# Attention maps turned by VectorE's 32x32 blocks and a round trip through DRAM, and the matrix engine's order around them written out by hand

## The chip, the cores and the metric

The kernel runs on one core of one Trainium2 chip. Times are device microseconds of the whole program on that core, taken over several executions; the profile shows one execution, instruction by instruction. The engines of the core work side by side, each through its own queue in order: TensorE (PE, with its weight loads as PEld), VectorE (DVE), ScalarE (ACT), GpSimd (POOL) and SyncE (SP), which here only issues transfers. A transfer can be issued from SP's, ACT's or POOL's queue; all of them end on the same 16 DMA engines.

## The reference, cut to what matters

Two layers, 256 tokens, width 1024, all in float32. Each layer normalises x, projects it, runs two token mixers, gates and merges them and projects back:

```python
proj = h @ w_in[l]                       # q_a k_a v_a ab z_a | q_b k_b v_b z_b | gate_a gate_b
y_a = gated_delta_branch(q_a, k_a, v_a, ab_a, z_a, ...)     # 8 heads of 128, both directions
# differential attention, 8 heads, two score maps of 64 channels each:
p = softmax(s); a = p[0] - lam * p[1]    # 256 x 256 for each head
o = einsum('bhqk,bhkd->bhqd', a, v)
y_b = rmsnorm(o) * (1 - lambda_init) * silu(z_b)
merged = sigmoid(gate_a) * (y_a @ w_pa[l]) + sigmoid(gate_b) * (y_b @ w_pb[l])
x = x + merged @ w_out[l]
```

The change concerns the map `a` of each head. It is made with queries on the partitions, but the product `a @ v` contracts over keys, so the map has to be turned before TensorE can use it.

## The kernel before, in words

**Projections.** The 256 tokens are two tiles (`m`) of 128. A projection of 512 columns (`proj_tm`, L315) runs over eight k-tiles of 128; each takes six matmuls of 512 columns: high x high, high x low and low x high part of the operands, for both token tiles. I call these six a **step**. Weights arrive in four loads of 512 KB a projection (`weights`, L273), each for two steps, on SP's queue (L304); ACT writes the rounded high part (L308), DVE the rest (L310). There are three buffers for raw weights and two each for the high and low parts, so each load waits until DVE is done with an older one.

**The stretch that the change is in.** In each layer, after the projections for q, k and v, TensorE works through ten projections of eight steps: zb0, zb1, za0, za1 (steps 0 to 31), gb0, gb1 (32 to 47), ga0, ga1 (48 to 63), pb0, pb1 (64 to 79). `place(at)` (L1158) names the last matmul of step `at`. Other work is put between these steps:

- **Attention.** `scores(h)` (L1053) makes the two score maps of head h at steps 3, 7, 11 ... 31; DVE takes the row maxima (L1069), ACT the exponentials and their sums (L1071), DVE combines the two maps (L1077) into `es[:, 0]`. `turn(h)` (L1081) turns the map: four TensorE transposes of 128x128 (L1088) into one PSUM bank and an ACT copy to `aT` (L1090). `attend(h)` (L1093) multiplies it with v (L1099). Turn and product of head h-1 stand beside the scores of head h, four steps later; head 7's stand at steps 34 and 39.
- **The delta rule's triangular inverse.** `substitute` (L865) solves 32x32 blocks on DVE (L870, L871), spread over the projections. `spread_blocks` (L873) makes a transposed copy (L874) and sends both to DRAM through POOL's queue (L878, `udr`). `merges(g)` (L897) for two groups g of four heads loads them back as `T64` (L905: group 0 through POOL's queue, group 1 through SP's) and into `U_` (L909, POOL's queue), and merges the blocks on TensorE from step 41 on (`y64p`, L923). `chunks(g)` (L976) follows from step 52 to 68.
- **Gating of the attention's output.** `gate_yb(i)` (L1236) scales half i of the heads (L1191), and `send`/`fetch` (L247, L254) turn it by DVE's block transpose (L249) and DRAM; `split_B` (L259) makes high and low parts for `pb`. It stands at the end of gb1 (i = 0) and at the end of ga0 (i = 1).

**What sets the order.** A scheduler orders each engine's instructions by priority in a simulated run. `behind(ins)` (L270) keeps an instruction behind another on its engine; `tc.high_priority` lifts it. TensorE's order between the steps comes from such pins and priorities.

**Buffers that matter.** `es` has two buffers (tag "w4a"), `aT` two (tag "w2a", L1084), score banks from head 2 on are the two of `ps_c`, turned maps and products with v use the two banks of `ps_m`. `ob` and the ga tiles share tag "eo", `vb` and the gb tiles share "ev".

**The turn by DVE and DRAM** already exists for v (`turn_squares` and `bounce`, L133 and L137): DVE transposes the 32x32 blocks in place, one transfer writes 256 KB to DRAM, four transfers of 64 KB read it back with the blocks in their new places, all on POOL's queue.

Of the kernel before, what the change touches and what calls it, by code (L numbers as in the profile page):

```python
# [17 lines left out]
P = 128  # L18
DM = 1024
KT = DM // P  # L20
SEQ = 256
# [28 lines left out]
def hybrid_encoder(  # L50
# [53 lines left out]
    mark = {}  # L104
# [53 lines left out]
    def norm_row(w_row, nm):  # L158
# [14 lines left out]
        for i in range(3):  # L173
            mm = T.matmul(wb[i > 0], one if i else tri[:, 0, :], hl[:, i - 1] if i else row,
                          start=i < 2, stop=i != 1)
            tc.keep_in_program_order(mm)
# [138 lines left out]
    def proj_tm(act, w, c0, n, evac, nm, places=(None,) * 4, spare=(), later=None, turned=(), between=None,  # L315
# [3 lines left out]
        for kt, hi, lo in weights(w, c0, n, nm, places, later=later, spare=spare, turned=turned, held=held,  # L319
                                  first=first, raws=raws):  # L320
            for m in range(NM):
                ts_ = slice(m * P, (m + 1) * P)
                o = accs[m][:, :n]
                T.matmul(o, act[kt // 4][:, 0, kt % 4, ts_], hi, start=kt == 0, stop=False)  # L324
                T.matmul(o, act[kt // 4][:, 0, kt % 4, ts_], lo, start=False, stop=False)  # L325
                mark["proj"] = T.matmul(o, act[kt // 4][:, 1, kt % 4, ts_], hi, start=False,  # L326
                                        stop=kt == KT - 1).ins
                mark["done", nm, kt] = mark["proj"]
        if between:
            between()  # L330
        for m in range(NM):
            evac(m, accs[m][:, :n])
# [76 lines left out]
    for _ in range(5):  # L409
        mm = T.matmul(idle[:, :P], ones, ones, start=True, stop=True)  # L410
        tc.keep_in_program_order(mm)
# [22 lines left out]
    for m in range(NM):  # L434
        mm = T.matmul(pos_p[:, m : m + 1], pos_r[:, m * P : (m + 1) * P], ones[0:1, 0:1], start=True, stop=True)
        mark["pos"] = mm.ins
        tc.keep_in_program_order(mm)
# [69 lines left out]
    for l in range(DEPTH):  # L507
# [86 lines left out]
        def qk_part(s_, i):  # L594
                def evac_qk(m, ps):
# [11 lines left out]
                    for b in range(4):  # L607
# [4 lines left out]
                proj_tm(hT, wl, (C_QB, C_KB)[s_] + 512 * i, 512, evac_qk, f"qk{l}{s_}{i}",  # L612
                        turned=(0, 1) if (s_, i) == (0, 1) else ())
# [170 lines left out]
        def gram(nm, g, c, slot, after=None):  # L784
            gp = (bank if slot else bank_c)(f"{nm}{l}{g}{c}")
            for j4 in range(4):
                kqh = kq[:, 4 * g + j4, c]
                with behind(after):
                    mark[nm, g, c] = T.matmul(gp[:, j4 * P : (j4 + 1) * P], kqh[:, 0, :], kqh[:, slot, :],
                                              start=True, stop=True).ins  # L790
# [35 lines left out]
        def weigh_q(g, c, after):  # L826
            bv = B[:, c, 4 * g : 4 * g + 4]
            with tc.high_priority(offset=HP):
                gp = gram("kq", g, c, 1, after)
# [554 lines left out]
```

## Time and profile before

| | us |
|---|---|
| median of three runs | 750.23 |
| fastest and slowest run | 749.87, 751.79 |
| the profiled execution, first to last instruction (its span) | 748.5 |

The profile gives a span and no time of its own for the execution that it shows; the median stands 1.7 us over that span.

| engine | busy us | share of span | instructions |
|---|---|---|---|
| PE (matmul) | 739.3 | 99% | 5176 |
| DVE | 586.5 | 78% | 1109 |
| ACT | 481.2 | 64% | 1022 |
| POOL | 139.5 | 19% | 221 |

In a view of groups, a row reads: line, engine and operation, result and operands, shape, count, then busy time in us and mean ns of one. A timeline row reads: start, duration, engine, line, operation, count, and in brackets the idle time before it and what ended it. In a table by stretch each engine's busy time is followed by its count, then the granted clock of TensorE, the DMA engines' busy share and GB/s. Matmul records overlap (each is shown with its run through the array), so what one costs in a stream is read from the distance between starts.

### The profile page before, as it was taken

Reading aid. Unit: us, or ns where it says so; the run is one execution under the profiler, and the core shown is the slowest. Engines: PE = TensorE matmul, PEld = TensorE weight load, DVE = VectorE, ACT = ScalarE, POOL = GpSimd, SP = SyncE. Lnnn points to the kernel's source line nnn. Section 1 sums busy time; section 2 is a strip of 40 time slices with the busy share of each in tenths; the row PEclk is TensorE's granted clock in tenths of the full one; section 3 lists DMA queues with packets and bytes.
Section 4 is the critical chain, followed back from the end, with each engine's and each line's share of the span. In section 5 each row is a group of like instructions: output and inputs, shape, how many; then the busy total and the mean of one; then the engine's idle time right before and its main releaser. Section 6 shows DMA issues by size and latency. Waiting matters only on the chain.

```text
span 748.5 us, 13917 instructions
## 1 busy us (share of the span) xinstructions
PE 739.3 (99%) x5176; PEld 641.7 (86%) x5176; DVE 586.5 (78%) x1109; ACT 481.2 (64%) x1022; POOL 139.5 (19%) x221
## 2 busy tenths in 40 slices
PE   8999999999999999999999999999999999999996
PEld 6999889987888889888889899889778888998885
DVE  8696898999985965578668779999999679537782
ACT  6757875667876576645456578555687757566552
POOL 6004110112023440100000150202110425301000
PEclk9999999999999999999999999999999999999999
DMA  8754566776667462567674466767666748335641
GB/s 260 239 170 169 170 179 198 209 211 193 208 177 186 145 184 84 171 200 247 199 232 133 128 192 180 219 176 230 195 171 195 197 133 229 95 114 201 220 141 57
DMA packets 73734, 135.46 MB, mean 181 GB/s; under 512 B 12944, under 2 KB 13921, under 8 KB 73666
## 3 DMA queue, kind: packets, MB, share of 16 engines
q1 hardware_dynamic: 64750, 113.65, 50.6%
q0 software_dynamic: 7936, 19.35, 8.7%
q10 hardware_dynamic: 980, 1.58, 0.6%
q8 instruction: 41, 0.67, 0.4%
q14 instruction: 27, 0.22, 0.1%
HBM read 125.53 MB, written 9.01 MB: 180 GB/s over the span
## 4 chain that ended last, share of the span: by engine, by line
PE 95%; ACT 2%; issue 1%; DVE 1%; DMA 1%; SPq 0%; POOLq 0%; POOL 0%; DVEq 0%; ACTq 0%
PE pp_vb L369 4%; PE pp_qk L325 4%; PE pp_qk L326 3%; PE pp_qk L324 3%; PE sc L1061 2%; PE pp_o L369 2%; PE pf_k L385 2%; PE pp_za L325 2%; PE pf_v L385 2%; PE pf_v L389 2%; PE pp_gb L324 2%; PE pp_gb L325 2%; PE pp_zb L324 2%; PE pf_q L387 2%; PE pf_k L387 2%; PE pf_v L387 2%
## 5 line engine op out<-in xcount | busy, mean ns | idle before, releaser
L325 PE MATMUL pp_qk<-lo_qk,hT 128*128 128x512 f32 x128 | 50.5, 395 | 0.3
L326 PE MATMUL pp_qk<-hi_qk,hT 128*128 128x512 f32 x128 | 50.0, 390 | 0.0
L310 DVE TENSOR_TENSOR lo_qk<-raw_qk,hi_qk 128x1024 fp32r<-128x1024 f32 x32 | 39.1, 1222 | 11.6 <-ACT hi_qk L308 11.4
L324 PE MATMUL pp_qk<-hi_qk,hT 128*128 128x512 f32 x128 | 45.1, 393 | 0.0
L308 ACT CAST hi_qk<-raw_qk 128x1024 fp32r<-128x1024 f32 x28 | 29.4, 1049 | 23.4 <-PE pp_qk L326 12.4
L1071 ACT ACTIVATE es<-sc,mx 128x256 f32<-128x256 f32 x64 | 29.6, 474 | 19.5 <-DVE mx L1069 19.5
L387 PE MATMUL pf_q<-hT,hi_q 128*128 128x256 f32 x128 | 36.1, 286 | 0.0
L385 PE MATMUL pf_k<-hT,hi_k 128*128 128x256 f32 x128 | 36.1, 287 | 0.0
L385 PE MATMUL pf_v<-hT,hi_v 128*128 128x256 f32 x128 | 35.9, 285 | 0.0
L387 PE MATMUL pf_v<-hT,hi_v 128*128 128x256 f32 x128 | 35.8, 284 | 0.0
L385 PE MATMUL pf_q<-hT,hi_q 128*128 128x256 f32 x128 | 35.8, 284 | 0.0
L387 PE MATMUL pf_k<-hT,hi_k 128*128 128x256 f32 x128 | 35.8, 284 | 0.0
L310 DVE TENSOR_TENSOR lo_pb<-raw_pb,hi_pb 128x1024 fp32r<-128x1024 f32 x16 | 19.6, 1225 | 20.5 <-ACT hi_pb L308 20.2
L389 PE MATMUL pf_q<-hT,lo_q 128*128 128x256 f32 x128 | 35.2, 288 | 0.0
L389 PE MATMUL pf_v<-hT,lo_v 128*128 128x256 f32 x128 | 34.6, 288 | 0.0
L389 PE MATMUL pf_k<-hT,lo_k 128*128 128x256 f32 x128 | 34.3, 284 | 0.0
L308 ACT CAST hi_pa<-raw_pa 128x1024 fp32r<-128x1024 f32 x16 | 16.8, 1053 | 22.3 <-PE pp_pa L326 16.1
L679 DVE SCALAR_TENSOR_TENSOR cvq<-pf_q,cw,cvq 128x254 f32<-128x254 f32 (+1 forms) x64 | 30.0, 479 | 0.9 <-ACT cvq L675 0.3
L679 DVE SCALAR_TENSOR_TENSOR cvv<-pf_v,cw,cvv 128x254 f32<-128x254 f32 (+1 forms) x64 | 30.1, 482 | 0.1
L679 DVE SCALAR_TENSOR_TENSOR cvk<-pf_k,cw,cvk 128x254 f32<-128x254 f32 (+1 forms) x64 | 29.0, 478 | 1.3 <-ACT cvk L675 0.6
L325 PEld LDWEIGHTS pp_qk<-lo_qk,hT 128*128 128x128 f32 x128 | 24.0, 188 | 6.6 <-DVE lo_qk L310 1.6
L310 DVE TENSOR_TENSOR lo_pa<-raw_pa,hi_pa 128x1024 fp32r<-128x1024 f32 x16 | 19.6, 1224 | 11.1 <-ACT hi_pa L308 11.1
(414 smaller groups left out, 2542.2 us busy)
## 6 DMA issues: line engine op xcount, KB each, us to landing
raw_qk<-in_w_in_dram SPq DMA_DIRECT2D x32, 512.0 KB, 3.8
raw_k<-in_w_in_dram SPq DMA_DIRECT2D x16, 512.0 KB, 4.7
raw_q<-in_w_in_dram SPq DMA_DIRECT2D x16, 512.0 KB, 3.7
raw_v<-in_w_in_dram SPq DMA_DIRECT2D x16, 512.0 KB, 3.8
raw_zb<-in_w_in_dram SPq DMA_DIRECT2D x16, 512.0 KB, 3.7
raw_za<-in_w_in_dram SPq DMA_DIRECT2D x16, 512.0 KB, 3.7
raw_ga<-in_w_in_dram SPq DMA_DIRECT2D x16, 512.0 KB, 4.4
raw_pb<-in_w_pb_dram SPq DMA_DIRECT2D x16, 512.0 KB, 3.8
```

What stands on the lines that cost most here:

```text
L308: high = (V.tensor_copy if kp in turned else S.copy)(hi[:, :, :n], raw[:, :, :n]).ins
L310: mark[nm, kp] = high, V.tensor_tensor(lo[:, :, :n], raw[:, :, :n], hi[:, :, :n].bitcast(F32), ALU.subtract).ins
L324: T.matmul(o, act[kt // 4][:, 0, kt % 4, ts_], hi, start=kt == 0, stop=False)
L325: T.matmul(o, act[kt // 4][:, 0, kt % 4, ts_], lo, start=False, stop=False)
L326: mark["proj"] = T.matmul(o, act[kt // 4][:, 1, kt % 4, ts_], hi, start=False, stop=kt == KT - 1).ins
L369: mark["proj"] = T.matmul(o, act[kt // 4][:, pa, kt % 4, ts_], ws[kt][1 + pw], start=kt == 0 and n_ == 0, stop=kt == KT - 1 and n_ == 2).ins
L385: T.matmul(o, hi[:, cs], act[kt // 4][:, 0, kt % 4, :], start=first, stop=False, skip_group_check=True)
L387: T.matmul(o, hi[:, cs], act[kt // 4][:, 1, kt % 4, :], start=False, stop=False, skip_group_check=True)
L389: T.matmul(o, lo[:, cs], act[kt // 4][:, 0, kt % 4, :], start=False, stop=done, skip_group_check=True)
L679: V.scalar_tensor_tensor(ca[:, o0:o1], acc[:, b, o0 + sft : o1 + sft], cw[:, j, cb : cb + 1], ca[:, o0:o1], ALU.mult, ALU.add)
L1061: mm = T.matmul(sp[n][:, qt * SEQ : (qt + 1) * SEQ], qkT[h // 4][rows, 0, h % 4, qt * P : (qt + 1) * P], qkT[h // 4][rows, 1, h % 4, :], s ...
L1071: S.activation(es[:, n, qt, :], spv[:, qt, :], AF.Exp, bias=mx[:, n, qt : qt + 1], accum_out=s_all[:, h, n, qt : qt + 1])
```

## The change

It does four things.

1. `turn` no longer uses TensorE. DVE transposes the map's 32x32 blocks into `es[:, 1]`, a transfer writes 256 KB to DRAM (`att`), and four transfers of 64 KB read it back as `aT`, all on POOL's queue, each kept behind the one before (`mark["queued"]`). The two query tiles lie interleaved, so TensorE reads the weights of `a @ v` with a step of two elements.
2. `a @ v` of head h stands at steps 20, 24, 28, 32, 36, 40, 43, 46, the scores at steps 6, 10 ... 34, so fourteen steps lie between them for heads 0 to 5, thirteen and twelve for the last two.
3. From zb0 to the end of pb1 every matmul made through `mm` is put behind the one before it; `drive` runs the projections step by step and runs the jobs that `plan` has put after a step. The steps of the merges, the chunk work and `weigh_q` keep their numbers.
4. `T64` of both groups and `U_` are loaded through SP's queue. `gate_yb(0)` and `gate_yb(1)` are issued at steps 54 and 58.

```diff
+    def mm(*args, **kw):
+        if mark["chain"] is None:
+            return T.matmul(*args, **kw)
+        with behind(mark["chain"]):
+            made = T.matmul(*args, **kw)
+        mark["chain"] = made.ins
+        return made
...
             for b in range(4):
                 co = 32 * (b % 2)
-                (nc.sync if g else G).dma_start(out=T64[blk(b), :, co : co + 32],
-                                                in_=udr[1, b, g].rearrange("t j i -> j t i"))
+                nc.sync.dma_start(out=T64[blk(b), :, co : co + 32],
+                                  in_=udr[1, b, g].rearrange("t j i -> j t i"))
             yield
             for b in range(4 if g == 0 else 0):
-                G.dma_start(out=U_[blk(b), :, :, blk(b)].rearrange("j g t i -> j (g t) i"),
+                nc.sync.dma_start(out=U_[blk(b), :, :, blk(b)].rearrange("j g t i -> j (g t) i"),
                                   in_=udr[0, b].rearrange("g t j i -> j (g t) i"))
...
-        def turn(h, es, at):
-            with tc.high_priority(offset=HP):
-                ap_ = bank(f"at{l}{h}")
-                aT = work.tile([P, NM, SEQ], F32, tag="w2a", name=f"aT{l}{h}", bufs=2)
-                for qt in range(NM):
-                    for kt in range(NM):
-                        with behind(at):
-                            mark["at", h] = T.transpose(ap_[:, kt * SEQ + qt * P : kt * SEQ + (qt + 1) * P],
-                                                        es[:, 0, qt, kt * P : (kt + 1) * P], ident).ins
-                S.copy(aT.rearrange("p k q -> p (k q)"), ap_)
-            return aT
...
+        def turn(h, es):
+            V.transpose(es[:, 1].rearrange("p k (j t q) -> p (k j) q t", j=4, q=2),
+                        es[:, 0].rearrange("p q (x t) -> p x q t", t=32))
+            dd = dram.tile([NM, 4, 32, 4, 64], F32, tag="att", name=f"att{l}{h}", bufs=4)
+            with behind(mark.get("queued")):
+                G.dma_start(out=dd.rearrange("k i t j r -> (i t) k (j r)"), in_=es[:, 1])
+            back = work.tile([P, NM, 4, 64], F32, tag="w2a", name=f"aT{l}{h}", bufs=2)
+            for j in range(4):
+                with behind(mark.get("queued")):
+                    mark["queued"] = G.dma_start(out=back[blk(j)].rearrange("t k i r -> t (k i) r"),
+                                                 in_=dd[:, :, :, j].rearrange("k i t r -> t (k i) r")).ins
+            aT[h] = back
+
+        def attend(h):
+            op_ = bank(f"av{l}{h}")
+            av = aT[h].rearrange("p k i (t q) -> p q k (i t)", q=2)
+            for qt in range(NM):
+                for kt in range(NM):
+                    mm(op_[:, qt * P : (qt + 1) * P], av[:, qt, kt],
+                       vb[h // 4][:, kt, h % 4 * P : h % 4 * P + P],
+                       start=kt == 0, stop=kt == NM - 1)
...
+        def attention(h):
+            turn(h, scores(h))
+
+        def drive(gens, first):
+            for n, gen in enumerate(gens):
+                for kt in range(KT):
+                    next(gen)
+                    for job in jobs.get(KT * (first + n) + kt, ()):
+                        job()
...
+        for h in range(NH):
+            plan((6, 10, 14, 18, 22, 26, 30, 34)[h], attention, h)
+        for h in range(NH):
+            plan((20, 24, 28, 32, 36, 40, 43, 46)[h], attend, h)
+        mark["chain"] = mark["proj"]
...
+            at = [mark[f"ga{l}1", m][1] if i else mark[f"ga{l}0", 2 + m][1] for m in range(NM)]
...
+        for n, at in enumerate((39, 42, 44, 47)):
+            plan(at, weigh_q, n // 2, n % 2)
         order = [(mg, 41), (mg[:1], 43), (mg[1:], 45), (mg, 48), (mg, 50)]
         order += [(ch[i : i + 1], at + i) for at in (52, 54, 57, 59, 62, 64, 67) for i in range(2)]
...
+        plan(54, gate_yb, 0)
+        plan(58, gate_yb, 1)
```

More of the change, by code (lines that the diff above doesn't have):

```diff
@@ L1093, in attend @@
[L1093 to L1101 removed]
+        aT = {}
@@ L1227, in hybrid_encoder @@
[L1227 to L1235 removed]
+        gtb, gta = [], []
@@ L1279, in hybrid_encoder @@
             gated(osb, za, ro, nw[:, 0:1], yaT, f"ya{l}", (m,))
-        branch(yaT, w_pa[l], gta, f"pa{l}")
+        for i in range(2):
+            full(branch(yaT, w_pa[l], gta, f"pa{l}", i))
         mT = pair(f"mT{l}")
```

225 lines of the change are left out of this document (93 added, 132 removed).

## The prediction, made before the change was run

> **What bounds the kernel now.** I read the page's busy times and chain first, then the table by stretch around the attention of layer 0, then the chain piece by piece there.
>
> ```profile
> span 748.5 us, 13917 instructions
> ...
> PE 739.3 (99%) x5176; PEld 641.7 (86%) x5176; DVE 586.5 (78%) x1109; ACT 481.2 (64%) x1022; POOL 139.5 (19%) x221
> ...
> PE 95%; ACT 2%; issue 1%; DVE 1%; DMA 1%; SPq 0%; POOLq 0%; POOL 0%; DVEq 0%; ACTq 0%
> 160.00:210.00 50.00, 50.00 (x266) 39.52 (x265) 48.28 (x107) 38.88 (x104) 5.46 (x10) 1.00 0.62 184
> 210.00:240.00 30.00, 30.00 (x164) 24.83 (x162) 20.62 (x37) 21.65 (x56) 9.27 (x16) 1.00 0.71 197
> 270.00:310.00 40.00, 40.00 (x284) 37.02 (x282) 17.46 (x34) 25.64 (x59) 7.57 (x11) 1.00 0.39 121
> ```
>
> The chain that ended last is TensorE for 95% of the span. In the three stretches it is busy all the time at the full granted clock (1.00). So a matmul taken out is worth its place in TensorE's stream, as long as nothing else becomes late. What could is also there: from 160 to 210 us DVE is busy 48.28 of 50 us, and the change gives DVE more to do just there. From 210 on DVE has room (20.62 of 30, then 17.46 of 40).
>
> **The transposes that go.** The chain shows what each instruction adds to the stream:
>
> ```profile
> 176.88 0.23 PE pp_zb L324
> 177.11 0.44 PE at L1088 x4
> 177.55 0.24 PE pp_zb L325
> ```
>
> A head's four transposes take 0.44 us between matmuls of 0.23. Eight heads in two layers: 16 x 0.44 = **7.0 us** off TensorE. A step is six matmuls, 6 x 0.23 = 1.4 us. Scores and products with v keep their number, so moving them costs nothing in itself; forcing the order by hand costs nothing where the data is there, and all of a wait where it is not, since TensorE cannot pass over.
>
> **The reads with a step of two elements.** No row shows TensorE reading weights so. The nearest rows are ACT and DVE with a step of four elements (16 bytes):
>
> ```profile
> L263 ACT ACTIVATE ybT<-zb,nw 128x512 fp32r<-128x512 f32 x8 | 9.9, 1241 | 0.0
> ...
> L1090 ACT COPY aT<-at 128x512 f32<-128x512 f32 x16 | 9.4, 585 | 0.0
> ...
> L244 ACT ACTIVATE yaT<-pt_ya,nw 128x512 fp32r<-128x512 f32 x8 | 5.1, 682 | 0.0
> L249 DVE STREAM_TRANSPOSE zb<-ob 128x512 f32<-128x512 f32 x8 | 8.4, 1092 | 0.1
> ...
> L135 DVE STREAM_TRANSPOSE tb_v<-thv 128x512 f32<-128x512 f32 x8 | 5.7, 712 | 0.0
> 204.61 0.89 PE av L1099 x8
> ...
> 212.68 0.89 PE av L1099 x8
> ```
>
> ACT's strided read (L263) takes 1.82 times the dense one from PSUM (L244); DVE's strided write (L249) 1.53 times the dense one (L135). A head's product is eight instructions in 0.89 us, 0.111 each, 128 in both layers. Bounds: 0, or 128 x 0.111 x 0.82 = 11.6 us. I see no reason for a gain. I take 0, because the step here is half of that in the slow rows, and keep 11.6 for the range. [...]
>
> **DVE and ACT.** DVE gains 16 block transposes with a write step of two: between the 0.712 us of L135 and the 1.092 of L249. I take 0.72, nearer to the dense row for the same reason as above; 5.8 us a layer. ACT loses 16 copies (L1090), 9.4 us; it was not full (38.88 of 50), so that is worth nothing. From 160 to 210 some six of the eight maps of a layer fall in: 48.28 + 6 x 0.72 = 52.6 us of work for 50 us, and TensorE wants to be through sooner. Something must slip. It need not be the weights: the block substitution is the work with time in hand, so what it feeds is late next (below). For casts that come late for TensorE the bounds are 0 and the excess of 2.6 us a layer; I take 0.4, 0.8 us in all.
>
> **The round trip.** That for v shows its length:
>
> ```profile
> 166.92 0.56 POOL L140 DMA_DIRECT2D bnc_v<-tb_v  x1 [11.61 <-DVE fstmp L870]
> 170.90 2.17 POOL L142 DMA_DIRECT2D tb_v<-bnc_v  x4 [3.42 <-DMA bnc_v<-tb_v]
> tb_v<-bnc_v POOLq DMA_DIRECT2D x32, 64.0 KB, 3.2
> ...
> T<-udr SPq DMA_DIRECT2D x8, 64.0 KB, 3.4
> 164.97 1.14 PE L1061 MATMUL sc<-qkT 64*128 64x256 f32 x8
> 174.56 0.89 DVE L1077 SCALAR_TENSOR_TENSOR es<-es,cc 128x256 f32<-128x256 f32 x2
> ```
>
> From the issue to the last byte back: 170.90 + 2.17 + 3.2 - 166.92 = 9.4 us. Before it stand the softmax (head 0, the slowest: 164.97 to 175.45, 10.5 us) and the transpose, 0.7: 20.6 us. The products of two heads stood 212.68 - 204.61 = 8.07 us apart, 7.6 without the transposes; that is four steps, so fourteen steps are some 26 us. Five are left over, so TensorE does not wait: 0. For heads 6 and 7 it is thirteen and twelve steps, filled with merge work.
>
> POOL's queue is the narrower place. Each of its five transfers for a head stands behind the one before, and the reads wait for the write: 166.92 to 173.07 is 6.2 us of every 7.6. Behind a waiting read stand the next head's write and, once a layer, the four `udr` writes. If a round trip held POOL longer than 7.6 us the delay would grow from head to head. The pieces read back are half as long as those of v; the traffic is 512 KB in 7.6 us, 67 GB/s beside 184, at a DMA share of 0.62; I take that as room enough.
>
> Four issues took 2.17 us while DVE was 97% busy. [...]
>
> **The merges' loads in SP's queue.** The path is: last block on DVE, `udr` written, `T64` read, `y64p` on TensorE.
>
> ```profile
> 212.54 1.10 DVE L874 COPY lt<-X 128x1024 f32<-128x1024 f32 x1
> 213.05 1.27 POOL L878 DMA_DIRECT2D udr<-X  x2 [25.55 <-issue]
> 222.38 2.73 SPq L905 DMA_DIRECT2D T<-udr  x4
> L905 SPq DMA_DIRECT2D T<-udr x8: 327/484/1247, 222.4 to 591.3; - x8
> L909 POOL DMA_DIRECT2D U__96<-udr x8: 791/796/814, 222.8 to 592.6; - x8
> 240.17 1.39 PE y64p L923 x102
> ```
>
> Six maps' transposes ahead of the last block put it 6 x 0.72 = 4.3 us later: SP's wait ends at 226.7. The eight `T64` loads take 8 x 0.484 = 3.9 us to issue and 3.4 to land: 234.0. `U_` follows with four issues; SP's price for one is not shown, with POOL's 0.796 and a landing like `T64`'s it is there by 237.2. TensorE: step 41 ends where 240.17 stood, less eight turns (3.5) and two products now later (1.8), plus ten matmuls of its own step and the one before that now come first (2.3): 237.2; `U_` is wanted two steps on, after 240. So the loads are 3 us early: 0. Behind them on SP stand the raw weights of gb1's second half and ga; TensorE wants them from step 44, and SP is free again near 234. With POOL's queue for the loads instead, they would stand behind the maps, so SP is what keeps this at 0.
>
> **Gating later.** It moves from a stretch where DVE is full to 270:310, where it has 22 us left.
>
> ```profile
> 245.76 0.35 DVE L1191 SCALAR_TENSOR_TENSOR ob<-ob,rb,zb 128x128 f32<-128x128 f32 x1
> 251.97 4.36 POOL L257 DMA_DIRECT2D zb<-bny_yb  x8 [1.25 <-DMA bny_yb<-zb]
> 275.96 3.57 PE sp L986 x32
> L324 PE MATMUL pp_pb<-hi_pb,ybT x64: 387/389/477, 299.1 to 695.3; 128*128 128x512 f32 x64
> ```
>
> From the first scaling of half 0 to its last piece back: 251.97 + 4.36 + 3.2 (the landing of `tb_v`'s reads) - 245.76 = 13.8 us; high and low parts for two tiles add some 3.7 (two of L263 at 1.241, and for the last low part, an estimate, as much as one of them). Step 54 stands at 275.96, step 64, the first that needs it, at 299.1: 23 us for 17.5. Nothing is gained, since TensorE waited for nothing at the old place, and nothing lost: 0, with 5 us of cover.
>
> **The sum.** 748.5 - 7.0 + 0.8 = 742.3 us of span. The page's execution has no time of its own; the median of the runs, 750.23, stands 1.7 over its span. 742.3 + 1.7 = **744.0 us**.
>
> **The rivals.**
>
> *The block substitution becomes the bound.* DVE is full, and the scheduler's simulated order may put more than the transposes ahead of the last block, or `udr` behind a waiting read of a map on POOL. The loads have 3 us left; each further microsecond costs TensorE one in each layer, at step 41. With 5 more us it is 2 x (5 - 3) = 4: 748.0 us; with 8 more, 754. For it speak the 48.28 of 50; against it that DVE has 9 us idle from 210 to 240 and that the substitution can be put ahead of softmax work.
>
> *The strided weight loads are slow (slower than before).* Place: the products with v, all 128 instructions. At ACT's factor they take 11.6 us more: 744.0 + 11.6 = 755.6. It decides from 7.0 / 128 = 55 ns for each load, half of the 111 ns pitch; at DVE's factor (0.111 x 0.53 x 128 = 7.5) it is 751.5, about no change. For it speak L263 and L249; against it that their step is twice as long.
>
> *The round trip holds POOL longer than a head takes.* At 8.9 us a head, which it is if each of the five issues takes 0.55 us more (half of an L249), it falls 1.3 us further behind with each, 10.4 by head 7, of which 5 are covered: 5.4 us a layer, 744.0 + 10.8 = 754.8. It decides from 7.6. For it speak longer queues of waits on POOL and pieces half as long; against it the 6.2. [...]
>
> *The change doesn't shorten TensorE's stream.* If what TensorE does is timed by the weights' casts, the 0.44 us are filled by waiting and the time stays at 750. Against it: matmuls follow one another at 0.23 us throughout the stretch.
>
> **How the numbers follow.** About 0.3% (2.3 us) is what a measurement of this kernel can tell from no change. Forecast, 742 to 747: 0.52. Substitution: 0.20, half of it faster, the rest the same but for 0.01. Strided loads: 0.11 (0.03 the same, 0.08 slower). POOL: 0.12 (0.02 the same, 0.10 slower). No shortening: 0.05, the same. Faster 0.52 + 0.10 = 0.62; the same 0.09 + 0.03 + 0.02 + 0.05 = 0.19; slower 0.19. The range of 741.5 to 756.0 starts a little under the full gain without late casts (743.2) and takes in the dear end of the strided loads; above it I leave the worse half of POOL's case, below it a few in a hundred.
>
> **What would show it.** Right: no transposes of `at` on PE, products still near 0.111 us an instruction in the chain, PE without idle time from zb0 to step 46, DVE's new transposes near 0.72 us, `T64` landed before `y64p`. Wrong: products with v at a pitch over 0.16 us; PE waiting at `av` for `aT`, at `y64p` for `T64` or at zb and za for `lo`; round trips on POOL over 7.6 us; raw weights of gb or ga issued late on SP behind the merges' loads.

## The result, and the profile after

| | us |
|---|---|
| before, median of four runs beside the changed kernel | 750.54 (749.87 to 751.79) |
| after, median of four runs | 756.16 (756.05 to 759.38) |
| ratio | 1.0085, 95% interval 1.0065 to 1.0105 |

The change costs 5.6 us. The forecast was 744.0 and a gain; the time lies 0.16 us above the range. That it lies so near the range's upper end is luck: that end was set by slow strided weight reads, and these cost 0.6 us. The profiled execution of the changed kernel was the longest of the four (759.38): beside the kernel before it has 1.6 us more ahead of zb in layer 0 and 1.7 behind the last matmul, where the change touches nothing, so lengths inside it are compared, not its end.

The page of the changed kernel: span, busy times, chain that ended last.

```profile
span 757.7 us, 13961 instructions
...
PE 741.5 (98%) x5112; PEld 638.7 (84%) x5112; DVE 595.0 (79%) x1125; ACT 473.0 (62%) x1006; POOL 178.6 (24%) x285
...
PE 78%; DVE 12%; issue 3%; ACT 3%; DMA 2%; POOL 0%; POOLq 0%; DVEq 0%; ACTq 0%
```

TensorE's 64 turn instructions are gone (5176 to 5112), but its share of the chain fell from 95% to 78%: VectorE holds 12% of it, ScalarE 3%, transfers 2%. The table by stretch says where (columns as before).

```profile
160.00:210.00 50.00, 48.98 (x234) 36.76 (x234) 49.93 (x110) 34.97 (x89) 15.37 (x26) 1.00 0.76 222
210.00:240.00 30.00, 30.00 (x276) 24.35 (x280) 25.05 (x45) 20.06 (x59) 15.46 (x27) 1.00 0.91 233
270.00:310.00 40.00, 40.00 (x267) 36.41 (x266) 28.64 (x55) 27.46 (x50) 16.73 (x26) 1.00 0.54 162
```

From 160 to 210 VectorE is busy 49.93 of 50 us and TensorE no longer is (48.98); from 210 to 240 the DMA share rose from 0.71 to 0.91.

The groups of the projections' matmuls in layer 0 have the first and last start of each; first of the kernel before, then of the changed one.

```profile
L324 PE MATMUL pp_zb<-hi_zb,hT x32: 388/389/499, 159.4 to 186.6; 128*128 128x512 f32 x32
L324 PE MATMUL pp_za<-hi_za,hT x32: 387/389/500, 187.7 to 219.5; 128*128 128x512 f32 x32
L324 PE MATMUL pp_gb<-hi_gb,hT x28: 388/390/501, 220.2 to 253.3; 128*128 128x512 f32 x28
L324 PE MATMUL pp_ga<-hi_ga,hT x32: 389/390/497, 254.8 to 295.9; 128*128 128x512 f32 x32
```

```profile
L110 PE MATMUL pp_zb<-hi_zb,hT x64: 387/393/504, 161.0 to 189.3; 128*128 128x512 f32 x64
L110 PE MATMUL pp_za<-hi_za,hT x64: 388/389/499, 189.5 to 219.9; 128*128 128x512 f32 x64
L110 PE MATMUL pp_gb<-hi_gb,hT x56: 388/392/795, 220.1 to 260.4; 128*128 128x512 f32 x56
L110 PE MATMUL pp_ga<-hi_ga,hT x58: 388/389/501, 261.5 to 299.9; 128*128 128x512 f32 x58
```

The distance from one first start to the next is the length of a stretch; all tables below are made so. Beside it stands the matrix work of the stretch, priced at the stream's rates (0.227 us a projection matmul, 96 in each; 1.06 for a head's scores; 0.44 a turn; 0.89 for a product and for each other group of eight 128x128 matmuls; gb without the merges).

| us, layer 0 / layer 1 | before | work | after | work |
|---|---|---|---|---|
| zb (steps 0 to 15) | 28.3 / 28.4 | 27.6 | 28.5 / 28.5 | 25.9 |
| za (16 to 31) | 32.5 / 32.4 | 31.4 | 30.6 / 30.6 | 28.7 |
| gb (32 to 47) | 34.6 / 34.7 | 30.0 | 41.4 / 37.4 | 30.9 |
| ga (48 to 63) | 44.3 / 44.3 | | 44.2 / 44.2 | |

Two things went wrong. In zb and za the work fell by 4.4 us and the time by 1.7. In gb it rose by 0.9 and the time by 6.8 and 2.7. From ga on nothing changed.

The wait in gb, chain of the changed kernel in layer 0 (projection matmuls left out):

```profile
229.34 0.93 PE av L110 x8
...
236.66 0.95 PE av L110 x8
237.60 0.39 issue
238.00 1.36 POOL aT L1087 x3
239.36 0.39 issue
239.75 7.04 DMA aT<-att
...
246.93 2.05 PE av L110 x8
```

Product 6 waits for its map, whose reading back is issued from 238.00 on; the last piece leaves at 239.75 and takes 7.04 us to land. Behind the wait TensorE is slow (same columns as the stretches above; the clock is the third number from the end):

```profile
240.00:244.00 4.00, 4.00 (x48) 3.20 (x34) 1.95 (x2) 1.59 (x3) 1.05 (x2) 1.00 1.07 330
244.00:248.00 4.00, 1.16 (x6) 1.10 (x6) 0.41 (x1) 0.00 (x0) 0.31 (x1) 0.77 0.62 200
248.00:254.00 6.00, 6.00 (x114) 5.19 (x114) 0.00 (x0) 3.32 (x11) 2.04 (x4) 0.58 0.32 68
254.00:262.00 8.00, 8.00 (x135) 6.83 (x134) 4.27 (x7) 5.82 (x15) 0.25 (x2) 1.00 0.25 68
```

2.8 us idle, then 6 us at a clock of 0.58, which is 2.5 us more (an estimate, 6 x 0.42). Why the map was late shows in POOL's timeline, with VectorE's transpose of map 6:

```profile
226.44 0.71 DVE L1079 STREAM_TRANSPOSE es<-es 128x512 f32<-128x512 f32 x1
```

```profile
221.00 2.34 POOL L1087 DMA_DIRECT2D aT<-att  x4 [1.22 <-DMA att<-es]
223.34 0.73 POOL L1083 DMA_DIRECT2D att<-es  x1
...
229.19 2.34 POOL L1087 DMA_DIRECT2D aT<-att  x4 [1.90 <-DMA att<-es]
231.52 0.72 POOL L1083 DMA_DIRECT2D att<-es  x1
...
238.00 2.34 POOL L1087 DMA_DIRECT2D aT<-att  x4 [5.75 <-PE av L110]
240.33 0.72 POOL L1083 DMA_DIRECT2D att<-es  x1
```

Map 6 is turned at 227.15 and written at 231.52: until then POOL stands at the landing of map 5 and issues its reads. From write to write it is 8.2 and 8.8 us here, where TensorE was to take a head every 7.6. POOL's order is not all of the wait. Map 6's own write landed 4.2 us after its issue, near 235.7, and its reading back left only at 238.00, 2.3 us later, where for heads 1 to 5 and 7 some 0.5 us lie between the two. The row puts this wait down to product 5, but the same 2.3 us stand at map 6 of layer 0 in the runs e2 and e4 below, where product 5 is not over when the read leaves. What POOL waits for there no view shows.

### The profile page after: what moved, and what is told of

Read it like the earlier page. It is cut to its first block, busy times and chain, and to the rows that moved or that the text cites. A ratio compares the mean times of both kernels' runs of the same rounds, so it can differ in the third digit from the quotient of the medians.

```text
span 757.7 us, 13961 instructions
## 1 busy us (share of the span) xinstructions
PE 741.5 (98%) x5112; PEld 638.7 (84%) x5112; DVE 595.0 (79%) x1125; ACT 473.0 (62%) x1006; POOL 178.6 (24%) x285
## 4 chain that ended last, share of the span: by engine, by line
PE 78%; DVE 12%; issue 3%; ACT 3%; DMA 2%; POOL 0%; POOLq 0%; DVEq 0%; ACTq 0%
PE pp_qk L108 8%; PE pp_ga L110 6%; PE pp_pb L110 6%; PE pp_pa L108 6%; PE pp_gb L110 4%; PE pp_vb L380 4%; PE pp_o L108 3%; PE pp_za L110 3%; PE pp_o L380 2%; PE pf_k L396 2%; PE pf_v L396 2%; PE pf_v L400 2%; PE pf_q L398 2%; PE pf_k L398 2%; PE pf_k L400 2%
## 5 line engine op out<-in xcount | busy, mean ns | idle before, releaser
L108 PE MATMUL pp_qk<-hi_qk,hT 128*128 128x512 f32 x256 | 81.1, 391 | 0.0
L108 PEld LDWEIGHTS pp_qk<-hi_qk,hT 128*128 128x128 f32 x256 | 47.4, 188 | 9.1
L1087 POOL DMA_DIRECT2D aT<-att x64 | 37.3, 590 | 61.7 <-PE pp_za L110 21.0
L321 DVE TENSOR_TENSOR lo_qk<-raw_qk,hi_qk 128x1024 fp32r<-128x1024 f32 x32 | 39.1, 1222 | 11.2 <-ACT hi_qk L319 11.0
L110 PE MATMUL pp_ga<-hi_ga,hT 128*128 128x512 f32 x128 | 45.6, 407 | 0.0
L110 PE MATMUL pp_za<-hi_za,hT 128*128 128x512 f32 x128 | 43.7, 402 | 0.0
L110 PE MATMUL pp_zb<-hi_zb,hT 128*128 128x512 f32 x128 | 42.8, 400 | 0.4 <-ACT es L1065 0.4
L110 PE MATMUL pp_pb<-hi_pb,ybT 128*128 128x512 f32 x128 | 42.7, 399 | 0.0
L110 PE MATMUL pp_gb<-hi_gb,hT 128*128 128x512 f32 x112 | 40.5, 414 | 0.0
L108 PE MATMUL pp_pa<-hi_pa,yaT 128*128 128x512 f32 x128 | 39.8, 389 | 0.0
L398 PE MATMUL pf_q<-hT,hi_q 128*128 128x256 f32 x128 | 36.1, 286 | 0.0
L396 PE MATMUL pf_v<-hT,hi_v 128*128 128x256 f32 x128 | 35.8, 285 | 0.0
L398 PE MATMUL pf_v<-hT,hi_v 128*128 128x256 f32 x128 | 35.8, 284 | 0.0
L396 PE MATMUL pf_q<-hT,hi_q 128*128 128x256 f32 x128 | 35.7, 284 | 0.0
L398 PE MATMUL pf_k<-hT,hi_k 128*128 128x256 f32 x128 | 35.7, 284 | 0.0
L400 PE MATMUL pf_v<-hT,lo_v 128*128 128x256 f32 x128 | 34.6, 288 | 0.0
L400 PE MATMUL pf_k<-hT,lo_k 128*128 128x256 f32 x128 | 34.3, 283 | 0.0
```

The costliest lines, as they stand in the source:

```text
L108: return T.matmul(*args, **kw)
L110: made = T.matmul(*args, **kw)
L321: mark[nm, kp] = high, V.tensor_tensor(lo[:, :, :n], raw[:, :, :n], hi[:, :, :n].bitcast(F32), ALU.subtract).ins
L396: T.matmul(o, hi[:, cs], act[kt // 4][:, 0, kt % 4, :], start=first, stop=False, skip_group_check=True)
L398: T.matmul(o, hi[:, cs], act[kt // 4][:, 1, kt % 4, :], start=False, stop=False, skip_group_check=True)
L400: T.matmul(o, lo[:, cs], act[kt // 4][:, 0, kt % 4, :], start=False, stop=done, skip_group_check=True)
```

## The experiments

Three theories at first. **L**: maps come late from POOL's chain and slow landings. **V**: VectorE, full in zb and za, hands weight parts over late. **O**: the hand-made order, SP's loads or the late gating cost by themselves. Each run has its ratio to the kernel before, measured beside it; that kernel's medians were 750.16 to 750.44.

### The trip, VectorE's part, the order, POOL's order

e1, no trip through DRAM:

```diff
-            dd = dram.tile(...)            # write, four reads
+            S.copy(back.rearrange("p k i r -> p (k i r)"), es[:, 1].rearrange("p k s -> p (k s)"))
```

> The round trip through DRAM is left out: ScalarE copies the block-transposed map to the place where it would be read back, so the 32x32 blocks are not moved to their new places. VectorE's transposes, the hand order, the merges' loads on SP and the late gating stay. Theory L (maps that come back late: POOL's chain and slow landings hold up product 6, 5.9 us between gb0 and ga0 of layer 0 and 1.9 us of layer 1): 756.2 - 7.8 = 748.4 us, and no wait at a product with v. Theory V (VectorE, full from zb to za, hands weight parts over late, some 2.7 us a layer): the same work is on VectorE, so about 756 if V is all there is; with both, 748.4 with a stretch from zb to gb still 59 us long. Theory O (the hand order, SP's loads or the late gating cost by themselves): 756.

e2, no block transpose:

```diff
-            V.transpose(es[:, 1]..., es[:, 0]...)
-                G.dma_start(out=dd..., in_=es[:, 1])
+                G.dma_start(out=dd..., in_=es[:, 0])
```

> VectorE's 32x32 block transpose of the maps is left out: the map as softmax leaves it goes through DRAM, so each block arrives unturned. The round trip on POOL's queue and all else stay. Theory V (VectorE full from zb to za): 756.2 - 2 x 2.7 = 750.8 us, with the stretch from zb to gb 56 to 57 us long instead of 59.1. Theory L (late maps): POOL's chain of 8.1 us a head stays, a map is 0.7 us earlier at most, so at least 754 us and the wait at product 6 still there. Theory O: 756.

e3, TensorE's turns in the hand-made order:

```diff
+            plan((14, 18, 22, 26, 30, 34, 37, 40)[h], turn, h)
-            plan((20, 24, 28, 32, 36, 40, 43, 46)[h], attend, h)
+            plan((16, 20, 24, 28, 32, 36, 39, 42)[h], attend, h)
```

> TensorE turns the maps again, inside the hand-made order: head h turned at steps 14, 18, 22, 26, 30, 34, 37, 40, its product two steps later, dense weights; no block transpose on VectorE and no round trip. The hand order, SP's loads of the merges and the late gating stay. Theory O (these three cost by themselves): above 752 us. Theories L and V (the cost sits in VectorE's transposes and the trip): 750.5 us as before the change or a little less, and no wait over 1 us between gb0 and ga0.

e4, POOL's order alone:

```diff
+            for h_ in ((0,), (1,), (), (2,), (3,), (4,), (5, 6), (7,))[h]:
+                fetch_map(h_)              # behind the write of map h
```

> Same work as the changed kernel; only the order on POOL's queue differs: from head 3 on a map is written before the map of the head before is read back, and head 6 is read back before head 7 is written, so POOL no longer stands at a write's landing while the next map is ready (4 to 6 us from map 3 on). Theory L: map 6 is written near 227.5 and read back by 242, two us before product 6 wants it; the wait and the lower clock behind it go, 756.2 - 7.8 = 748.4 us at best, 751 if the landings stay slow. Theories V and O: 756, since VectorE and the order have what they had.

| run | us | ratio, interval | zb | za | gb |
|---|---|---|---|---|---|
| e1 no trip | 751.6 | 1.0016 (1.0005 to 1.0027) | 28.4 / 28.4 | 31.3 / 32.6 | 36.2 / 36.2 |
| e2 no block transpose | 750.7 | 1.0005 (0.999 to 1.002) | 27.8 / 27.9 | 30.5 / 31.3 | 36.1 / 37.7 |
| e3 TensorE turns | 754.1 | 1.0049 (1.003 to 1.0067) | 28.3 / 28.3 | 32.9 / 33.0 | 36.3 / 36.3 |
| e4 early writes | 751.8 | 1.0016 (1.0006 to 1.0026) | 28.5 / 28.5 | 30.6 / 30.6 | 36.9 / 36.8 |

e4 decides for L in gb: with the same work, 4.4 us are back, all of them there. POOL's timeline of e4:

```profile
226.42 0.72 POOL L1083 DMA_DIRECT2D att<-es  x1
227.14 2.32 POOL L1094 DMA_DIRECT2D aT<-att  x4
233.69 2.32 POOL L1094 DMA_DIRECT2D aT<-att  x4 [4.23 <-PE pp_gb L110]
```

Map 6 is written 5.1 us earlier and read back 4.3 us earlier (1.5 of each because this execution reached zb at 159.5, not at 161.0); no product waits for a map.

e2 is a miss for L. It asked for 754 us or more with the wait at product 6 still there; the run has 750.7, as V said, and in layer 0 no wait at a product. POOL's writes stand 8.3 us apart on average (8.1 in the changed kernel), but the first is issued 19.4 us after the start of zb, in the changed kernel 22.4; map 6 is read back 75.0 us after it, in the changed kernel 77.0, and is just in time. So VectorE's transposes and POOL's order share that wait, and taking out either ends it.

Still, e1, e2 and e4 all stop at or above the kernel before, and e3 is as much a surprise: with TensorE's turns and none of the new work on VectorE and POOL it is 3.9 us slower. Its zb is as long as before although 1.3 us of matrix work (one turn, one product) moved out of it, and its gb is 1.7 longer, with 1.3 us more work there. Hence a fourth theory, **F**: a floor in zb, where other engines set the pace and matrix work is free.

### Is work in zb free?

e5, on e4:

```diff
+        def more(at):
+            op_ = bank(f"mo{l}{at}")
+            for n in range(4):
+                mm(op_[:, n % 4 * P : n % 4 * P + P], ident, ident, start=True, stop=True)
+        for at in (7, 12, 37, 38):
+            plan(at, more, at)
```

> Beside the version with early writes (751.8 us): per layer 8 added matrix instructions of 128x128 fp32 (two passes of 0.111 us each, 1.78 us together) after steps 7 and 12, in zb, and as many after steps 37 and 38, in gb; nothing reads them. Theory F (a floor: from zb0 to zb1 VectorE's work sets the pace, 28.3 to 28.5 us whatever TensorE has to do, so matrix work there is free and its removal is worth nothing): zb stays within 0.5 us of 28.5, gb grows by 1.8: 755.4 us in all. Theory O (the hand-made order makes waits of its own, whatever VectorE does): both grow, zb to 30.3: 759 us.

e6, on e4:

```diff
-                V.tensor_reduce(mx[:, n, :], spv, AX.X, ALU.max, negate=True)
-                    S.activation(es[:, n, qt, :], spv[:, qt, :], AF.Exp, bias=mx[:, n, qt : qt + 1],
+                    S.activation(es[:, n, qt, :], spv[:, qt, :], AF.Exp, scale=0.01,
```

> Beside the version with early writes (751.8 us): the row maxima and their subtraction are left out (scores times 0.01 inside the exponential, so that nothing overflows); that takes two VectorE reductions of 0.61 us from each head, some 3.7 us from zb. TensorE's work and order are the same. Theory F: zb falls from 28.5 to about 26.5 us, za from 30.6 to 29.5: 746 us. Theory O: zb and za stay, 751.8 us.

e7, on e3, and e8, a mixture:

```diff
+            plan((12, 18, 20, 24, 28, 32, 36, 41)[h], attend, h)      # e7
+            plan((10, 15, 18, 22, 25, 30, 33, 37)[h], turn, h)
+            plan((3, 7, 12, 18, 22, 25, 30, 33)[h], attention, h)
...
+            if h in (0, 1, 6, 7):                                      # e8
+                maps[h] = scores(h)        # turned by TensorE after steps 10, 15, 37, 40
```

> As the run with TensorE's turns in the hand-made order (754.1 us), but scores, turns and products at the steps that they had before the change (scores after steps 3, 7, 12, ..., turn of head 0 after 10, product of head 0 after 12, of head 7 after 41). SP's loads for the merges and the late gating stay. Theory F (what was lost there is matrix work moved out of zb, where it was under VectorE's cover, to gb): 750.2 to 751 us, zb 28.4 and gb 34.6 to 35. Theory O (hand order, SP's loads or late gating cost by themselves): 753 us or more.

> TensorE turns heads 0, 1 (under VectorE's cover in zb), 6 and 7 (whose round trip would be late); VectorE and DRAM turn heads 2 to 5. Scores after steps 3, 7, 12, 17, 21, 25, 29, 33, products after 12, 18, 27, 31, 35, 39, 41, 43; the loads of the merges in the queues that they had before the change. Theory F with L (late maps): zb 28.3 as before, za 30.2 instead of 32.5, gb 36 instead of 34.6 (one product more, the last two turns there as before): 748.3 us, under both kernels. If the hand order costs by itself (O): 751 us or more.

| run | us | ratio, interval | zb | za | gb |
|---|---|---|---|---|---|
| e5 more matrix work | 756.4 | 1.0080 (1.0065 to 1.0095) | 28.8 / 28.8 | 30.4 / 30.4 | 39.1 / 38.7 |
| e6 no row maxima | 752.7 | 1.0037 (1.0023 to 1.0052) | 28.2 / 28.2 | 31.2 / 32.8 | 35.9 / 35.8 |
| e7 same places | 754.1 | 1.0051 (1.0036 to 1.0066) | 28.8 / 28.8 | 34.3 / 34.3 | 34.5 / 34.5 |
| e8 mixture | 761.6 | 1.0149 (1.0134 to 1.0164) | 28.7 / 28.7 | 36.5 / 37.6 | 35.7 / 35.7 |

e5 shows the floor: 1.78 us of added work cost 0.3 in zb and 2.2 and 1.9 in gb. e6 contradicts the simple form of it, that VectorE's amount of work is the pace. The low casts in VectorE's timeline, e4 first, then e6:

```profile
174.95 1.20 DVE L321 TENSOR_TENSOR lo_zb<-raw_zb,hi_zb 128x1024 fp32r<-128x1024 f32 x1
```

```profile
175.04 1.18 DVE L321 TENSOR_TENSOR lo_zb<-raw_zb,hi_zb 128x1024 fp32r<-128x1024 f32 x1
```

Of the maxima that e6 takes from zb (3.7 us) two, 1.4 us, stood ahead of the sixth cast, and it comes no earlier. In e4 it starts 0.07 us after ScalarE's high cast of the same weights, which ends at 174.88; in e6, whose zb starts 0.7 us sooner, that one ends at 174.12 and the low cast comes 0.92 us behind it, since the scheduler has put the combining and the block transpose of a map ahead of it. The whole run is 0.9 us slower than e4, with za 0.6 and 2.2 longer. So what counted here was the cast's place in two in-order queues, more than how full VectorE's is.

e7 and e8 miss. In e7 gb is back at 34.5, as F said, but za is 1.8 us longer, and the time is the one that theory O named (753 or more): the hand-made order, or SP's loads and the late gating that stay with it, cost something even at the scheduler's places. e8 loses 4 to 5 us in za. Waits of e7, then of e8, between 159 and 262 us (total, times, longest):

```profile
PE at L1084 <- DVE es L1071: 1.1, 1, 1.1
```

```profile
PE av L110 <- ACT aT L1101: 3.6, 1, 3.6
```

In e7 the turn of head 4 stands three steps behind its scores and the map isn't there; in e8 ScalarE's copy of head 1's turned map stands behind the exponentials of head 3. TensorE, in a fixed order, stands still in both. A place copied from the scheduler's order isn't safe once the rest is fixed by hand.

### The floor of zb, SP's queue, and two mixtures

e9, on e4:

```diff
+                    other = raw[:, :, :n] if nm[:2] in ("zb", "za") else hi[:, :, :n].bitcast(F32)
+                    mark[nm, kp] = high, V.tensor_tensor(lo[:, :, :n], raw[:, :, :n], other, ALU.subtract).ins
```

> Beside the version with early writes (751.8 us): in zb and za the low part is made from the raw weights alone (raw minus raw), so VectorE's cast no longer waits for ScalarE's high part; the low parts of these weights are left out of the product by it. VectorE, ScalarE and TensorE keep every instruction. Theory F2 (a chain of latencies: with two buffers a weight pair's high cast starts only when TensorE has left the buffer, 1.05 us, then the low cast behind it, 1.2 us and what stands before it on VectorE, so in zb a pair takes 3.5 us of which TensorE has work for 3.2): zb falls from 28.5 to about 26.5 us, za from 30.6 to 29.5, 751.8 - 6 = 746 us. Theory F1 (VectorE's order and load set the pace): zb within 0.5 us of 28.5, 751 to 752 us.

e10, on e4: `G.dma_start` for `U_`, chained between the reads of maps 5 and 6.

> The version with early writes, but the four loads of U_ stand on POOL's queue, between the reading back of maps 5 and 6, instead of on SP's. Theory S (on SP they hold back the last raw weights of gb by 4.7 us, whose cast on ScalarE stands ahead of the merge's copy, so TensorE waits 0.8 us at zt in layer 0 and 0.4 at z in layer 1): raw_gb is issued near 231.5 instead of 236.1, these waits go, 750.5 us. If SP's queue costs nothing: 751.8 us. If the loads hold POOL past 233.7, map 6 is late again and it is above 752.

e11, on the kernel before: heads 6 and 7 through VectorE and DRAM, products pinned behind steps 43 and 46. e12, on e10: head 0 turned by TensorE.

> The kernel before, with its scheduler's order, in which only heads 6 and 7 are turned by VectorE and DRAM; their products are pinned behind steps 43 and 46. The turns that go lie in gb (and its edge), where TensorE sets the pace, not in zb. Theory F with L: 4 turns of 0.44 us go at full price, 750.3 - 1.8 = 748.5 us, since two trips a layer do not queue on POOL. If the trip or the later products make a wait of their own, it is 750 us or more.

> The version with early writes and U_ on POOL, in which TensorE turns head 0 again, early: scores after step 3, turn after 10, product after 12, all in zb; heads 1 to 7 as there. Theory F: these 1.33 us of matrix work are nearly free in zb (28.8 us at most), and the product leaves za or gb at full price: 0.7 us a layer less than that version, 749.2 us if that one gives 750.5. If work in zb costs its full price: 750.5 + 0.9 = 751.4 us.

| run | us | ratio, interval | zb | za | gb |
|---|---|---|---|---|---|
| e9 low casts alone | 750.8 | 1.0010 (0.9999 to 1.0021) | 28.1 / 28.1 | 29.8 / 29.8 | 37.5 / 36.6 |
| e10 U_ on POOL | 751.1 | 1.0008 (0.9998 to 1.0017) | 28.4 / 28.4 | 30.6 / 30.6 | 37.2 / 37.2 |
| e11 heads 6, 7 | 751.5 | 1.0014 (1.0004 to 1.0023) | 28.4 / 28.3 | 32.4 / 32.5 | 33.7 / 33.8 |
| e12 head 0 | 750.9 | 1.0002 (0.9992 to 1.0011) | 29.3 / 29.2 | 29.8 / 29.8 | 36.6 / 36.7 |

e9: the chain of two casts alone isn't the floor either (0.4 in zb, 0.8 in za). With it gone the next wait shows:

```profile
PE pp_zb L110 <- ACT es L1065: 0.9, 1, 0.9
```

that is, the high cast behind ScalarE's exponentials.

e10: in e4 TensorE waits 0.8 us at `zt`. Theory S put this down to the merge's copy on ScalarE, behind a cast that waits for raw weights; the view gives no releaser. With `U_` off SP's queue the load is issued earlier and lands hardly earlier. The wait in e4, then load and cast in e4 and in e10:

```profile
245.17 0.21 PE L110 MATMUL zt<-U__96,y 32*32 32x32 f32 x1 [0.80 <-issue]
```

```profile
236.06 1.09 SPq L315 DMA_DIRECT2D raw_gb<-in_w_in_dram  x1
...
242.23 1.05 ACT L319 CAST hi_gb<-raw_gb 128x1024 fp32r<-128x1024 f32 x1 [4.83 <-DMA raw_gb<-in_w_in_dram]
```

```profile
233.25 0.39 SPq L315 DMA_DIRECT2D raw_gb<-in_w_in_dram  x1
...
241.22 1.05 ACT L319 CAST hi_gb<-raw_gb 128x1024 fp32r<-128x1024 f32 x1 [3.49 <-DMA raw_gb<-in_w_in_dram]
```

The issue is 2.8 us earlier, the cast only 1.0, 8 us behind the issue; the wait at `zt` stays 0.8 us, so theory S is not borne out and that wait is open. The place in SP's queue was not the limit of the load; it shares the 16 DMA engines with the maps' and the merges' pieces (their queues' shares of these engines add up to 102.5% from 234 to 236 us and 106.4% from 236 to 238).

e11: gb is 0.9 shorter, ga 1.6 and 2.2 longer (45.9 and 46.5). The scheduler put the products behind steps 47 and 48, not 43 and 46, and so the last one into ga (chain of e11):

```profile
252.28 0.47 PE av L1118 x4
...
256.10 1.14 PE av L1118 x8
```

So gb has two turns and a product less, 1.8 us, and is 0.9 shorter; ga has a product more, 0.9, and is 1.6 and 2.2 longer. Where the rest went is open. e12: the product left za (0.8 gained), but zb rose by 0.8, not the 0.3 that e5 showed; its scores stand three steps earlier as well, and which of the two it was wasn't tried.

### The floor taken together, and the idea at its best

e13, on e4: e6, e9 and the transposes of e2 left out together. e14: no turn at all, in the changed kernel's order. e15: e14 with products at steps 16, 20, 24, 28, 32, 36, 39, 42, as in e3.

```diff
-            V.transpose(es[:, 1]..., es[:, 0]...)                      # e14
-            dd = dram.tile(...)
+            S.copy(back.rearrange("p k i r -> p (k i r)"), es[:, 0].rearrange("p k s -> p (k s)"))
```

> The version with early writes (751.8 us) without the row maxima, without the block transposes of the maps and with low casts of zb and za that don't wait for the high ones (all three left out of the computation); trips, order and TensorE's work stay. Theory F3 (the floor of zb is the casts' place behind softmax work on VectorE and ScalarE, all of it together): zb 26.5, za 29.5 instead of 28.5 and 30.6, 751.8 - 2 x 3.1 = 745.6 us. If the three together give no more than about one of them (zb 28, za 30), the floor is something else, such as the raw weights or ScalarE alone: 750 us or more.

> The changed kernel with no turn of the maps at all (left out): neither TensorE's nor VectorE's, no trip through DRAM; ScalarE copies the map as it is to the place of the turned one. Order, products' places, the merges' loads on SP and the late gating stay. This is the most that the idea could give: by the forecast's own sum 742 to 744 us. By theory F (what is taken from TensorE in zb saves nothing there, and the products come to gb at full price): zb 27.9, za 30.5, gb 36, together 1.0 us a layer under before: 748 us.

> As the run with no turn at all, but the products with v ten steps behind the scores instead of fourteen (steps 16, 20, 24, 28, 32, 36, 39, 42): one product a layer more in za, one less in gb. Theory F (matrix work in gb costs its full price, in zb and za about half): gb 35.1 instead of 36, za 30.9 instead of 30.5, 1 us less than that run in all. If moved products cost the same everywhere (the forecast's step): the same time.

| run | us | ratio, interval | zb | za | gb |
|---|---|---|---|---|---|
| e13 light softmax | 747.5 | 0.9965 (0.9952 to 0.9978) | 26.7 / 26.7 | 30.4 / 31.1 | 35.8 / 35.8 |
| e14 free turn | 748.9 | 0.9982 (0.9972 to 0.9991) | 27.9 / 27.9 | 31.1 / 31.1 | 36.1 / 36.1 |
| e15 free turn, earlier products | 747.7 | 0.9966 (0.9953 to 0.9978) | 27.9 / 27.9 | 31.3 / 31.3 | 35.1 / 35.1 |

e13 lifts the floor: zb is 26.7 for 25.9 us of matrix work. So softmax work and casts on VectorE and ScalarE make the floor, the three causes together (1.8 us; alone the transposes gave 0.7 in e2, the cast's dependence 0.4 in e9, the maxima 0.3 in e6). Whether it is the casts' place behind that work or its amount, e13 doesn't separate, since it takes away both. The forecast of 745.6 us missed: in za 29.5 was forecast, and 30.4 and 31.1 came, with waits of 0.3 and 1.0 us for a high cast on ScalarE; the rest is open.

e14 is the answer to what the idea could give: with a turn that costs TensorE, VectorE and POOL nothing (ScalarE still copies each map) the order of the changed kernel is 1.3 us faster than before, not 7. e15 shows the place alone: the same instructions, products four steps earlier, 1.2 us less, one product's worth out of gb in each layer (36.1 to 35.1) and nearly free in za (31.1 to 31.3).

No version that leaves nothing out was faster than the kernel before.

## Why the prediction was wrong, step by step

The runs differ by one thing from line to line (from e3 to e15 by two: the products also read with a step of two), so they make a sum of medians. Each median is good to about 1 us; the last column has, as a check, what zb, za and gb of both layers changed by in the profiled executions:

| from | to | us | stretches |
|---|---|---|---|
| before, 750.2 | e3: the hand order and its places, TensorE still turning | +3.9 | +4.2 |
| e3, 754.1 | e15: the turns gone | -6.4 | -6.5 |
| e15, 747.7 | e14: products four steps later | +1.2 | +1.6 |
| e14, 748.9 | e1: VectorE's transposes | +2.7 | +2.9 |
| e1, 751.6 | e4: the trip for ScalarE's copy, writes early | +0.2 | -1.2 |
| e4, 751.8 | after: POOL in the order write, read, write, read | +4.4 | +5.1 |
| | together | +6.0 | +6.1 |

What a line is worth depends on what else is there. Taken out of the changed kernel alone, VectorE's transposes are worth 5.5 us (e2), the trip 4.5 with ScalarE's copy in its place (e1), and POOL's order 4.4 (e4). Transposes and trip together are worth 7.3 (e14), less than their sum, since the wait at product 6 is gone in each of these runs.

- **The transposes that go, -7.0**: right in mechanism and nearly in size, 6.4 where TensorE's order stays as it is. The one turn that leaves zb from e3 to e15 is worth 0.4 us even there, so zb's floor is no fixed length: it moves with the order of the work on VectorE and ScalarE.
- **"Scores and products with v keep their number, so moving them costs nothing in itself; forcing the order by hand costs nothing where the data is there"**: this step failed, with 3.9 + 1.2 = 5.1 us. The 3.9 are 1.3 us a layer of matrix work that came to gb without zb getting shorter, and 0.7 a layer that no single wait explains. Here a matmul was worth its place only where TensorE set the pace (e5: 1.78 us of added work cost 0.3 us in zb, 2.2 and 1.9 in gb). In zb the work of before (27.6 us) and what casts allow (27.8 to 28.8 in all runs but e12 and e13) lie within about a microsecond of each other. Before the change TensorE was busy all the time in zb (28.30 of 28.30 us in layer 0, at a granted clock of 1.00), and that hid the second limit just beneath. Two turns and a product, 1.8 us, left zb and gave at most 0.4 there (e14); with the later places gb got two more products, 1.8 us, for two turns less, 0.9, and pays for them in full (e5, e15). The fourth rival, weights' casts that time TensorE, was given 0.05; it holds in the main in zb, in part in za, and not in gb. Its argument (matmuls follow one another at 0.23 us) excludes a limit above the work, not one right under it.
- **VectorE, +0.8**: mis-sized. Duration right (0.72 taken, 0.704 in the group's row below); the cost is 2.7 us, 1.35 a layer, inside the bounds of 0 to 2.6 (5.5 with the trip behind them, as said above). The weight loads of TensorE wait for low casts of zb and za in the changed kernel's layer 0 (total, times, longest).

```profile
L1079 DVE STREAM_TRANSPOSE es<-es 128x512 f32<-128x512 f32 x16 | 11.3, 704 | 0.0
```

```profile
PEld pp_zb L110 <- DVE lo_zb L321: 1.5, 2, 1.1
...
PEld pp_za L110 <- DVE lo_za L321: 0.9, 2, 0.5
```

- **The round trip, 0**: failed, 4.6 us, of which 4.4 are POOL's order (the 0.2 can't be told from nothing). POOL's hold on a head was put at 6.2 us of every 7.6 and measured 8.2 (0.72 + 5.1 + 2.34). The issues were nearly right (0.72 and 2.34 for 0.56 and 2.17). The wait for the write was mis-sized: from the end of its issue to the first read 3.42 us in the row for v, 5.1 here (median of the eight in layer 0); and a read lands in 4.6 where 3.2 was taken. From the view of transfers, 176 to 262 us (times, size, median us to landing):

```profile
att<-es POOLq DMA_DIRECT2D x8, 256.0 KB, 5.1
aT<-att POOLq DMA_DIRECT2D x32, 64.0 KB, 4.6
```

The third rival had this mechanism and the point from which it decides (7.6); it looked for issues 0.55 us longer each, an estimate of the author's that no run shows: the five took 0.72 + 2.34 = 3.06 us, 0.33 more in all than the 2.73 of the rows for v. That its 754.8 is near the measured time is luck: it had 10.8 us for POOL on top of the full gain. "67 GB/s beside 184" was no room: the DMA share rose to 0.91.
- **Reads with a step of two, 0**: 0.93 us for eight instructions in place of 0.89 (chain rows above), 16 x 0.04 = 0.6 us in all, far from the 11.6 of the dear end. It is part of e14's 748.9 too. VectorE's transposes took 0.704 us with such a write step (row above), 0.712 with a dense one (L135 of the kernel before).
- **SP's loads and the late gating, 0**: `T64` and `U_` came about when they were reckoned, so the block substitution, the first rival, did not become the bound. SP's timeline and TensorE's wait there:

```profile
227.32 5.66 SPq L913 DMA_DIRECT2D T<-udr  x6
233.03 3.43 SPq L917 DMA_DIRECT2D U__96<-udr  x4
236.56 0.51 SPq L315 DMA_DIRECT2D raw_gb<-in_w_in_dram  x1
```

```profile
PEld y64p L110 <- DMA U__96<-udr: 0.4, 1, 0.4
```

Six `T64` loads took 5.66 us to issue where 2.9 were reckoned, and the raw load behind them left at 236.56 for "near 234"; but e10 shows that leaving earlier hardly helps. Gating cost nothing: ga and pb are as long as before.

Open: 0.7 us a layer of e3's loss, in za and gb; how much of the hand order's cost is the places and how much the fixed order itself, since e7 is no faster than e3; the floor in za; the 2.3 us ahead of map 6's read; and how much of the wait at product 6 is the low clock behind it in other executions than the profiled one.

## What to carry to other kernels

An engine that is busy all the time can hide a second limit right beneath it (here TensorE in zb: 27.6 us of matrix work, and casts that allow 27.8 to 28.8): before taking work off it, ask stretch by stretch what the next limit is, add some dummy work there and see whether it costs anything. Moving work from a stretch with such a floor to one without cost its full price here, even though no instruction was added (e15 to e14, a product a layer out of za into gb: 1.0 us more in gb, 0.2 less in za). The round trip through one in-order queue held that queue for the landing of its write as well as for its issues (5.1 us of the 8.2 of a head); put the next write ahead of the read that waits (4.4 us in e4), and size landings at the DMA load of the changed kernel (medians of 5.1 and 4.6 us), not at that of the old one (3.4 and 3.2).

## What the runs showed of the hardware that was not expected

After 2.8 us without matmuls the clock granted to TensorE was 0.58 from 248 to 254 us; layer 1's waits of 0.9 us in all left it at 1.00 (table by stretch of the changed kernel):

```profile
612.00:620.00 8.00, 7.09 (x129) 5.90 (x128) 2.36 (x2) 4.73 (x14) 1.61 (x3) 1.00 0.77 229
```

And a 512 KB load took 8 us from its issue to its cast in e10. The raw loads of gb in the kernel before landed in 4.9 (median, last column):

```profile
raw_gb<-in_w_in_dram SPq DMA_DIRECT2D x12, 512.0 KB, 4.9
```

The maps' and merges' pieces beside it on the same engines are the likely reason; that was not tried by itself.
